# RWKV operands: a block's intermediate values in PSUM, affine steps on ScalarE

## The chip, the cores and the metric

The kernel runs on one core of a Trainium2 chip. The time is device microseconds from the start of the program to its end on that core; lower is better. Five engines work side by side: PE (TensorE, matrix products), DVE (VectorE), ACT (ScalarE), POOL (GpSimd) and SP (SyncE, which issues the transfers). Each takes its instructions in its own fixed order and waits for semaphores that others raise. SBUF is the on-chip memory of all engines, PSUM the one that PE writes its products to; in this kernel PSUM is eight banks of 128 partitions x 512 floats.

## The reference, cut to what matters

One layer of a hybrid backbone: one input projection feeds three branches, mLSTM, RWKV-7 and RG-LRU, whose results are gated and projected out. There are 2304 tokens of width 1024: 256 of context and 2048 of latent. The change concerns what RWKV needs for each token before its recurrence can run:

```
log_w = -RWKV_DECAY_SCALE * sigmoid(r_w0 + einsum('btdr,drc->btdc', tanh(wl), r_w2))
a     = sigmoid(r_a0 + einsum('btdr,drc->btdc', al, r_a2))
kt    = k * (1.0 + (a - 1.0) * r_ka)
bvec  = kh * a
# then, per head and direction, token by token:
S = S * w - (S kh) b + v kt;   y = S r        # w = exp(log_w)
```

The kernel runs the recurrence in chunks of 64 tokens. For that it needs, in each chunk, the running sum of log_w (its exponential is called E here, its inverse cs), and kh, r, b and kt multiplied by E or by its inverse. sigmoid(x) is computed as 0.5 tanh(x/2) + 0.5.

## The kernel before, in words

The program is written as generators that a small planner (class `Flow`) runs on an estimated clock. A generator issues its instructions and yields a delay or an event; the planner picks the next one by rank and due time. The order of PE's instructions is the order in which the planner reached them. The order on the other engines is that of a list scheduler, within the dependencies; semaphores are placed from the dependencies between tiles. All PSUM tiles of the program come from one pool `ps` of eight banks, which are handed on in turn, so that a new tile waits until the last reader of an older one is done. PE fills the time between the branches' work with the input projection (tiles `pp_...`).

`derive()` (L833 to L1063) makes the RWKV operands. There are 54 blocks of 256 tokens of one head pair and direction, in 7 stages (6 blocks in the first, 8 in each other one). Three `worker()` generators (`NW` = 3) take blocks in turn, and the tile `KB`, which holds a block's four results, has three buffers. For one block, `block()` does the following.

- PE: `pw`, four matmuls of 256 columns into one PSUM bank: the decay's argument in the first half, a's in the second.
- ACT: Tanh of each half into `KB` (L950, L952).
- DVE: the affine step 0.5 x + 0.5 into `cs` (L955), then the scan, the running sum over each chunk (L956).
- ACT: E = exp(-cs) into `E` (L957), one of two tiles with a column of ones ahead of each chunk, and the inverse into `cs` (L958).
- The a's half, scaled and shifted by two pointers, becomes two parts of `KB`: one on DVE (L959), one on ACT (L960).
- DVE: four products: `KB` halves by z (L965, 512 columns), kh by E (L967), r by E (L969 forward, L971 backward), and both halves by the inverse (L972, 512 columns).
- SP: three transfers of `KB` to the array `CH` in DRAM; ACT: a copy of E's last column into `Dall` (L977).

After a planned delay the worker lets PE multiply parts of the block with each other (`pt`, 16 matmuls), and ACT reads the bank six times into `DG` and `OF` (L1007 to L1009). When the blocks of a stage are in, DVE transposes `DG` into `W` (L1049), and POOL solves 32 triangular systems by a recursion of 30 steps of two instructions (L1058, L1060), masked at its start (L1050). DVE transposes the result back (L1030, L1031) and copies it (L1034), and PE and ACT merge it (`pY`, L909, `pX`, L918) before it goes to `CH`. When the last stage is merged, `derive()` is over and the mLSTM branch begins.

Of the kernel before, what the change touches and what calls it, by code (L numbers as in the profile page):

```python
# [9 lines left out]
F32 = mybir.dt.float32  # L10
F32R = mybir.dt.float32r
BF16 = mybir.dt.bfloat16
AF = mybir.ActivationFunctionType
ALU = mybir.AluOpType
# [11 lines left out]
DECAY = 0.6065306597126334  # L26
# [806 lines left out]
def derive(X, dv):  # L833
    nc, vec, hv, CH, F = X["nc"], X["vec"], X["hv"], X["CH"], X["F"]
    V = _VI
    NW, LOAD, LAT = 3, 10000.0, 11000.0
    sm = dv.tile([128, 256], BF16, name="sm")
# [5 lines left out]
    for s, (on, off) in enumerate(((slice(0, 64), slice(64, 128)), (slice(64, 128), slice(0, 64)))):  # L843
        nc.vector.memset(ab[on, 2 * s:2 * s + 2], 0.5)
        nc.vector.tensor_scalar(ab[off, 2 * s], ka[off], 0.5, None, op0=ALU.mult)
        nc.vector.tensor_scalar(ab[off, 2 * s + 1], ka[off], -0.5, 1.0, op0=ALU.mult, op1=ALU.add)
    Es = []
    for i in range(2):
        Es.append(dv.tile([128, 4, 65], F32, name=f"E{i}"))
        nc.gpsimd.memset(Es[i][:, :, 0:1], 1.0)  # L850
    CP = TP // 64
# [5 lines left out]
    n, per = 256, 4  # L857
# [16 lines left out]
    taken = [Event() for _ in stages]  # L874
    ahead, cnt = [], [0]

# [52 lines left out]
    def block():  # L929

        _, sid, p, d, i0, l0, nm, wa, z = ahead.pop(0)
        E = Es[cnt[0] % 2]
        cnt[0] += 1
        bw = d == 1
# [8 lines left out]
        def tok(x):  # L943

            v = x.rearrange("p (c j) -> p c j", j=64) if len(x.shape) == 2 else x
            return v[:, ::-1, ::-1] if bw else v
        sa = KB[:, :, 0]
        sw = KB[:, :, 1]
        i = V[f"w0_{d}{p}"]
        nc.scalar.activation(sw, pw[:, 0].rearrange("p (c j) -> p c j", j=64), AF.Tanh, scale=0.5, bias=hv[:, i:i + 1])  # L950
        i = V[f"a0_{d}{p}"]
        nc.scalar.activation(sa, pw[:, 1].rearrange("p (c j) -> p c j", j=64), AF.Tanh, scale=0.5, bias=hv[:, i:i + 1])  # L952
        cf = dv.tile([128, 256], F32, tag="cs", name=f"cs{nm}", bufs=2)
        cs = cf.rearrange("p (c j) -> p c j", j=64)
        nc.vector.tensor_scalar(cs, tok(sw), 0.5, 0.5, op0=ALU.mult, op1=ALU.add)  # L955
        nc.vector.tensor_tensor_scan(out=cf, data0=sm, data1=cf, initial=0.0, op0=ALU.mult, op1=ALU.add)  # L956
        nc.scalar.activation(E[:, :, 1:65], cs, AF.Exp, scale=-DECAY)  # L957
        nc.scalar.activation(cs, cs, AF.Exp, scale=DECAY)  # L958
        nc.vector.tensor_scalar(KB[:, :, 2], tok(sa), ab[:, 0, p:p + 1], ab[:, 1, p:p + 1], op0=ALU.mult, op1=ALU.add)  # L959
        nc.scalar.activation(KB[:, :, 3], tok(sa), AF.Identity, scale=ab[:, 2, p:p + 1], bias=ab[:, 3, p:p + 1])  # L960
        z4 = z[:, 2:4].rearrange("p a (c j) -> p c a j", j=64)
        if bw:
            z4 = z4[:, ::-1, :, ::-1]
        k = KB[:, :, 2:4]
        nc.vector.tensor_tensor(out=k, in0=k, in1=z4, op=ALU.mult)  # L965
        kh, r3 = tok(z[:, 0]), z[:, 1].rearrange("p (c j) -> p c j", j=64)
        nc.vector.tensor_tensor(out=KB[:, :, 1], in0=E[:, :, 0:64], in1=kh, op=ALU.mult)  # L967
        if bw:
            nc.vector.tensor_tensor(out=KB[:, :, 0], in0=E[:, :, 64:0:-1], in1=r3[:, ::-1], op=ALU.mult)  # L969
        else:  # L970
            nc.vector.tensor_tensor(out=KB[:, :, 0], in0=E[:, :, 1:65], in1=r3, op=ALU.mult)  # L971
        nc.vector.tensor_tensor(out=k, in0=cs[:, :, None].to_broadcast([128, 4, 2, 64]), in1=k, op=ALU.mult)  # L972
        ch = CH[p, d][:, i0:i0 + per].rearrange("p c (a j) -> p c a j", j=64)
        nc.sync.dma_start(ch[0:64, :, 2:6], KB[0:64])
        nc.sync.dma_start(ch[64:128, :, 0:2], KB[64:128, :, 2:4])
        nc.sync.dma_start(ch[64:128, :, 2:4], KB[64:128, :, 0:2])
        nc.scalar.activation(X["Dall"][:, p, d, i0:i0 + per], E[:, :, 64], AF.Copy)  # L977
        if d:
# [992 lines left out]
```

## Time and profile before

| | us |
|---|---|
| median of 3 runs | 2057.64 (2053.56 to 2067.47) |
| the profiled execution, its time | 2059.59 |
| its span on the core | 2057.9 |
| PE busy in the span | 1801.6 (88%) |
| DVE busy | 1367.0 (66%) |
| ACT busy | 977.6 (48%) |
| POOL busy | 795.0 (39%) |
| blocks of `derive()`, first scan to last product | 644 to 968 |

The span is that of one execution taken by the hardware profiler. An engine is busy while it executes an instruction; waiting is idle time. A row that says that A waited for B names what ended the wait last. In the order rows below, a bracket names the queues and engines whose semaphores an instruction waits for; Activation is ACT.

### The profile page before, as it was taken

The page shows a single profiled execution, that of the slowest core. Times are in us where ns is not written, and L with a number is a line of the kernel's source. Part 1 is how long each engine was busy: PE and PEld are TensorE (multiplying, and loading weights), DVE is VectorE, ACT ScalarE, POOL GpSimd, SP SyncE. Part 2 cuts the span into 40 slices and gives each one's busy share as a digit, 9 for nine tenths or more (in the row PEclk, how much of TensorE's full clock was granted, in tenths as well). Part 3 has the DMA queues.
Part 4 walks back from the last instruction along what each step waited for, and adds up shares of the span by engine and source line. Part 5 has one row for each costly group of instructions (what it writes and reads, how often), then busy time and mean ns, then how long its engine had stood idle before and what let it go on. Part 6 is the DMA issues. An engine that isn't in the chain of part 4 may idle for free. (4 is left out here: it accounts for less than half of the span.)

```text
span 2057.9 us, 46221 instructions
## 1 busy us (share of the span) xinstructions
PE 1801.6 (88%) x16648; PEld 1201.0 (58%) x16778; DVE 1367.0 (66%) x3271; ACT 977.6 (48%) x2634; POOL 795.0 (39%) x1200
## 2 busy tenths in 40 slices
PE   5899999999999878788899798878778788999996
PEld 3555655656666556555566565555555556777774
DVE  3747366777643898998324766647885576777774
ACT  5732446565434667776242545542332233444442
POOL 0210011112110688888722444342653232444442
PEclk9899999999999988889999899989888999999997
DMA  7343344564548778887254666645986545576662
GB/s 284 118 142 90 126 123 133 153 168 148 132 127 247 215 207 223 225 214 176 80 154 135 188 171 170 171 118 154 292 268 193 164 136 149 163 196 203 197 190 72
DMA packets 353370, 350.60 MB, mean 170 GB/s; under 512 B 109554, under 2 KB 294978, under 8 KB 350728
## 3 DMA queue, kind: packets, MB, share of 16 engines
q1 hardware_dynamic: 353142, 347.65, 59.2%
q8 instruction: 133, 2.18, 0.5%
q14 instruction: 95, 0.78, 0.1%
HBM read 211.18 MB, written 136.37 MB: 169 GB/s over the span
## 5 line engine op out<-in xcount | busy, mean ns | idle before, releaser
L1635 POOL TENSOR_SCALAR sd<-cg,Dall 128x128 f32<-128x128 f32 x210 | 135.8, 654 | 267.1 <-DVE cg L1659 164.0
L1659 DVE SCALAR_TENSOR_TENSOR cg<-cq,Dall,sd 64x64 f32<-64x64 f32 x408 | 114.5, 281 | 46.4 <-PE cq L168 36.6
L1060 POOL TENSOR_TENSOR W<-W,tmp 128x30 f32<-128x30 f32 (+14 forms) x210 | 139.0, 662 | 16.1
L1058 POOL TENSOR_TENSOR tmp<-W 128x30 f32<-128x30 f32 (+14 forms) x210 | 133.0, 633 | 15.9
L168 PE MATMUL cq<-cg,bt 128*64 128x64 f32 x840 | 68.5, 246 | 49.7 <-DVE cg L1644 44.6
L1283 ACT ACTIVATE nb<-nb,aT 128x128 f32<-128x128 f32 x216 | 71.6, 393 | 82.5 <-DMA nb<-nm_d 72.4
L168 PE MATMUL cq<-cg 128*64 128x64 f32 x1728 | 92.9, 230 | 8.2 <-DVE cg L1659 8.2
L168 PEld LDWEIGHTS cq<-cg,bt 128*64 128x64 f32 x840 | 44.1, 142 | 84.9 <-DVE cg L1644 54.8
L168 PE MATMUL ga<-cg 64*64 64x128 f32 (+1 forms) x864 | 76.9, 270 | 16.9 <-DMA cg<-ch 16.9
L1630 ACT ACTIVATE q<-cq 128x64 f32<-128x64 f32 x216 | 45.5, 223 | 95.7 <-PE cq L168 92.3
L1592 DVE TENSOR_TENSOR cg<-gb,rmask 64x256 f32<-64x256 f32 x108 | 44.7, 413 | 66.3 <-PE gb L168 61.1
L168 PEld LDWEIGHTS cq<-cg 128*64 128x64 f32 x1728 | 72.9, 141 | 24.3 <-issue 9.5
L168 PE MATMUL pz<-owhi,zhi 128*128 128x512 f32 x180 | 82.1, 456 | 4.5 <-ACT zhi L1822 4.5
L1598 ACT ACTIVATE bt<-ga 128x256 f32<-128x256 f32 x108 | 41.3, 383 | 87.0 <-DVE G L1595 83.4
L168 PE MATMUL pt<-KB 64*64 64x64 f32 x864 | 41.9, 244 | 45.7 <-DVE KB L972 45.6
L1284 POOL TENSOR_SCALAR_AFFINE_SELECT nb<-nb 128x256 f32<-128x256 f32 x108 | 44.8, 421 | 93.0 <-ACT nb L1283 63.6
L168 PE MATMUL gb<-cg 64*64 64x128 f32 (+1 forms) x864 | 75.7, 270 | 0.9 <-DMA cg<-ch 0.9
L168 PE MATMUL pz<-owhi,zlo 128*128 128x512 f32 x180 | 73.5, 409 | 3.3 <-DVE zlo L1823 3.3
L168 PE MATMUL pz<-owlo,zhi 128*128 128x512 f32 x180 | 72.9, 405 | 0.0
L168 PEld LDWEIGHTS ga<-cg 64*64 64x64 f32 x864 | 48.2, 142 | 41.9 <-issue 27.9
L168 PE MATMUL cq<-q,cg 128*64 128x64 f32 x864 | 59.4, 236 | 9.9 <-ACT q L1630 9.9
L168 PE MATMUL pp_v<-hhi,whi_v 128*128 128x512 f32 (+1 forms) x120 | 67.4, 562 | 0.3 <-ACT whi_v L514 0.3
(511 smaller groups left out, 6180.0 us busy)
## 6 DMA issues: line engine op xcount, KB each, us to landing
cg<-ch SPq DMA_DIRECT2D x216, 192.0 KB
wa<-wa SPq DMA_DIRECT2D x54, 256.0 KB
z<-z SPq DMA_DIRECT2D x27, 512.0 KB
ch<-KB SPq DMA_DIRECT2D x108, 128.0 KB
ch<-KB SPq DMA_DIRECT2D x54, 256.0 KB
nb<-nm_d SPq DMA_DIRECT2D x108, 128.0 KB
lr<-L SPq DMA_DIRECT2D x16, 768.0 KB
lL<-lr SPq DMA_DIRECT2D x16, 768.0 KB
```

The costliest lines, as they stand in the source:

```text
L168: self.nc.tensor.matmul(out, lhsT, rhs, start=start, stop=stop, **kw)
L1058: nc.gpsimd.tensor_tensor(out=tv, in0=W[:, j + 1:32, j:j + 1].to_broadcast([128, m, j]), in1=W[:, j:j + 1, 0:j].to_broadcast([128, m, j]), ...
L1060: nc.gpsimd.tensor_tensor(out=W[:, j + 1:32, 0:j], in0=W[:, j + 1:32, 0:j], in1=tv, op=ALU.add)
L1283: nc.scalar.activation(nb[:, d, j], nb[:, d, j], AF.Exp, bias=aT[:, c, d, 2 * p + j:2 * p + j + 1])
L1284: nc.gpsimd.affine_select(out=nb[:, d], in_=nb[:, d], pattern=[[0, 2], [1 - 2 * d, 128]], base=0, channel_multiplier=-1 + 2 * d, compare_o ...
L1592: nc.vector.tensor_tensor(out=cg[o, :, RK[h]], in0=src[o], in1=mask[o, d].rearrange("p a c -> p (a c)")[:, None].to_broadcast([64, 2, 128] ...
L1598: nc.scalar.activation(bt, ga[:, 1], AF.Copy)
L1630: nc.scalar.activation(q, qk, AF.Copy, scale=-1.0)
L1635: nc.gpsimd.tensor_scalar(sd, cg.rearrange("p (n c) -> p n c", c=64)[:, 0::9], Dk, None, op0=ALU.mult)
L1659: nc.vector.scalar_tensor_tensor(out=nxt[h][b], in0=ps[b], scalar=Dk[b], in1=sd[b, 1 - h], op0=ALU.mult, op1=ALU.add)
```

## The change

A block's intermediate values stay in PSUM. Both Tanh write in place into `pw`, the affine step is an ACT instruction of its own on that bank (L945 of the changed kernel), the scan reads it (L950), and E replaces the decay's half of `pw` (L956). Both ka-steps run on ACT, from `pw` into a new PSUM tile `kb` (L954, twice), in which DVE multiplies by z (L961); the last product reads `cs` from SBUF and `kb` from PSUM into `KB` (L969). So each DVE product has one operand in PSUM. The tiles E0 and E1 with their columns of ones go; the product of kh by E is now 63 columns of each chunk (L964), and the first column is copied (L963). `Dall` is read from `pw` (L974). PE's matmuls, the transfers, the stages, the workers and the planner's delays are as before, and PE's instructions stand in the same order.

```diff
--- before.py
+++ after.py
@@ -844,10 +844,6 @@
         nc.vector.memset(ab[on, 2 * s:2 * s + 2], 0.5)
         nc.vector.tensor_scalar(ab[off, 2 * s], ka[off], 0.5, None, op0=ALU.mult)
         nc.vector.tensor_scalar(ab[off, 2 * s + 1], ka[off], -0.5, 1.0, op0=ALU.mult, op1=ALU.add)
-    Es = []
-    for i in range(2):
-        Es.append(dv.tile([128, 4, 65], F32, name=f"E{i}"))
-        nc.gpsimd.memset(Es[i][:, :, 0:1], 1.0)
     CP = TP // 64
 
     stages = [[(p, d, 0, CP, CP * (2 * p + d)) for p in range(3) for d in range(2)]]
@@ -872,7 +868,7 @@
     full = [Event() for _ in stages]
     merged = [Event() for _ in stages]
     taken = [Event() for _ in stages]
-    ahead, cnt = [], [0]
+    ahead = []
 
     def load(lat=LOAD):
 
@@ -929,8 +925,6 @@
     def block():
 
         _, sid, p, d, i0, l0, nm, wa, z = ahead.pop(0)
-        E = Es[cnt[0] % 2]
-        cnt[0] += 1
         bw = d == 1
         pw = X["ps"].tile([128, 2, 256], F32, tag="b", name=f"pw{nm}")
         for j in range(2):
@@ -944,37 +938,40 @@
 
             v = x.rearrange("p (c j) -> p c j", j=64) if len(x.shape) == 2 else x
             return v[:, ::-1, ::-1] if bw else v
-        sa = KB[:, :, 0]
-        sw = KB[:, :, 1]
+
+        sw, sa = pw[:, 0], pw[:, 1]
         i = V[f"w0_{d}{p}"]
-        nc.scalar.activation(sw, pw[:, 0].rearrange("p (c j) -> p c j", j=64), AF.Tanh, scale=0.5, bias=hv[:, i:i + 1])
+        nc.scalar.activation(sw, sw, AF.Tanh, scale=0.5, bias=hv[:, i:i + 1])
+        nc.scalar.activation(sw, sw, AF.Copy, scale=0.5, bias=0.5)
         i = V[f"a0_{d}{p}"]
-        nc.scalar.activation(sa, pw[:, 1].rearrange("p (c j) -> p c j", j=64), AF.Tanh, scale=0.5, bias=hv[:, i:i + 1])
+        nc.scalar.activation(sa, sa, AF.Tanh, scale=0.5, bias=hv[:, i:i + 1])
         cf = dv.tile([128, 256], F32, tag="cs", name=f"cs{nm}", bufs=2)
         cs = cf.rearrange("p (c j) -> p c j", j=64)
-        nc.vector.tensor_scalar(cs, tok(sw), 0.5, 0.5, op0=ALU.mult, op1=ALU.add)
-        nc.vector.tensor_tensor_scan(out=cf, data0=sm, data1=cf, initial=0.0, op0=ALU.mult, op1=ALU.add)
-        nc.scalar.activation(E[:, :, 1:65], cs, AF.Exp, scale=-DECAY)
-        nc.scalar.activation(cs, cs, AF.Exp, scale=DECAY)
-        nc.vector.tensor_scalar(KB[:, :, 2], tok(sa), ab[:, 0, p:p + 1], ab[:, 1, p:p + 1], op0=ALU.mult, op1=ALU.add)
-        nc.scalar.activation(KB[:, :, 3], tok(sa), AF.Identity, scale=ab[:, 2, p:p + 1], bias=ab[:, 3, p:p + 1])
+        nc.vector.tensor_tensor_scan(out=cf, data0=sm, data1=sw[:, ::-1] if bw else sw, initial=0.0, op0=ALU.mult, op1=ALU.add)
+        k = X["ps"].tile([128, 4, 2, 64], F32, tag="b", name=f"kb{nm}")
+        sat = tok(sa)
+        for s in range(2):
+            nc.scalar.activation(k[:, :, s], sat, AF.Identity, scale=ab[:, 2 * s, p:p + 1], bias=ab[:, 2 * s + 1, p:p + 1])
+        E = sw.rearrange("p (c j) -> p c j", j=64)
+        nc.scalar.activation(sw, cf, AF.Exp, scale=-DECAY)
+        nc.scalar.activation(cf, cf, AF.Exp, scale=DECAY)
         z4 = z[:, 2:4].rearrange("p a (c j) -> p c a j", j=64)
         if bw:
             z4 = z4[:, ::-1, :, ::-1]
-        k = KB[:, :, 2:4]
         nc.vector.tensor_tensor(out=k, in0=k, in1=z4, op=ALU.mult)
         kh, r3 = tok(z[:, 0]), z[:, 1].rearrange("p (c j) -> p c j", j=64)
-        nc.vector.tensor_tensor(out=KB[:, :, 1], in0=E[:, :, 0:64], in1=kh, op=ALU.mult)
+        nc.vector.tensor_copy(KB[:, :, 1, 0:1], kh[:, :, 0:1])
+        nc.vector.tensor_tensor(out=KB[:, :, 1, 1:64], in0=E[:, :, 0:63], in1=kh[:, :, 1:64], op=ALU.mult)
         if bw:
-            nc.vector.tensor_tensor(out=KB[:, :, 0], in0=E[:, :, 64:0:-1], in1=r3[:, ::-1], op=ALU.mult)
+            nc.vector.tensor_tensor(out=KB[:, :, 0], in0=E[:, :, ::-1], in1=r3[:, ::-1], op=ALU.mult)
         else:
-            nc.vector.tensor_tensor(out=KB[:, :, 0], in0=E[:, :, 1:65], in1=r3, op=ALU.mult)
-        nc.vector.tensor_tensor(out=k, in0=cs[:, :, None].to_broadcast([128, 4, 2, 64]), in1=k, op=ALU.mult)
+            nc.vector.tensor_tensor(out=KB[:, :, 0], in0=E, in1=r3, op=ALU.mult)
+        nc.vector.tensor_tensor(out=KB[:, :, 2:4], in0=cs[:, :, None].to_broadcast([128, 4, 2, 64]), in1=k, op=ALU.mult)
         ch = CH[p, d][:, i0:i0 + per].rearrange("p c (a j) -> p c a j", j=64)
         nc.sync.dma_start(ch[0:64, :, 2:6], KB[0:64])
         nc.sync.dma_start(ch[64:128, :, 0:2], KB[64:128, :, 2:4])
         nc.sync.dma_start(ch[64:128, :, 2:4], KB[64:128, :, 0:2])
-        nc.scalar.activation(X["Dall"][:, p, d, i0:i0 + per], E[:, :, 64], AF.Copy)
+        nc.scalar.activation(X["Dall"][:, p, d, i0:i0 + per], E[:, :, 63], AF.Copy)
         if d:
             load()
         return sid, l0, nm, KB
```

ACT's queue at block 1_10241 (stage 1), before; `pY` belongs to the merge of the stage before:

```order
L950 ACTIVATE KB_1_10241_7548<-pw_1_10241_7543,hv 128x4x64 [waits DMAHW5_49,DMAHW6_49,DMAHW2_49,PE_49]
L952 ACTIVATE KB_1_10241_7548<-pw_1_10241_7543,hv 128x4x64
L960 ACTIVATE KB_1_10241_7548<-KB_1_10241_7548,rab 128x4x64 [waits Activation_49]
L957 ACTIVATE E_5316<-cs_1_10241_7551 128x4x64 [waits DVE_49]
L958 ACTIVATE cs_1_10241_7551<-cs_1_10241_7551 128x256 [waits Activation_49]
L977 ACTIVATE Dall<-E_5316 128x4
L909 ACTIVATE OF_6058<-pY_7474 32x512 [waits PE_49]
L909 ACTIVATE OF_6058<-pY_7474 32x512
```

After, at the same block:

```order
L944 ACTIVATE pw_1_10241_7597<-pw_1_10241_7597,hv 128x256 [waits PE_49]
L945 ACTIVATE pw_1_10241_7597<-pw_1_10241_7597 128x256 [waits Activation_49]
L947 ACTIVATE pw_1_10241_7597<-pw_1_10241_7597,hv 128x256 [waits Activation_49]
L954 ACTIVATE kb_1_10241_7608<-pw_1_10241_7597,rab 128x4x64 [waits DVE_49]
L954 ACTIVATE kb_1_10241_7608<-pw_1_10241_7597,rab 128x4x64 [waits Activation_49]
L956 ACTIVATE pw_1_10241_7597<-cs_1_10241_7606 128x256 [waits Activation_49]
L957 ACTIVATE cs_1_10241_7606<-cs_1_10241_7606 128x256 [waits Activation_49]
L974 ACTIVATE Dall<-pw_1_10241_7597 128x4 [waits DVE_49]
L905 ACTIVATE OF_6072<-pY_7528 32x512 [waits PE_49]
```

The ka-step has moved from ahead of the scan's result to behind it (L960 waited for ACT alone, the first L954 waits for DVE), each instruction now waits for the one ahead of it, and the copy into `Dall` waits for DVE.

DVE's queue at the same block, before:

```order
L955 TENSOR_SCALAR cs_1_10241_7551<-KB_1_10241_7548 128x256 [waits Activation_49]
L959 TENSOR_SCALAR KB_1_10241_7548<-KB_1_10241_7548,rab 128x4x64 [waits DMAHW5_49,DMAHW2_49,DMAHW6_49,PE_49,Activation_49]
L956 SCALAR_TENSOR_TENSOR cs_1_10241_7551<-sm,cs_1_10241_7551 128x256 [waits DVE_49]
L965 TENSOR_TENSOR KB_1_10241_7548<-KB_1_10241_7548,z_1_1024_7295 128x4x128 [waits DVE_49,Activation_49]
L967 TENSOR_TENSOR KB_1_10241_7548<-E_5316,z_1_1024_7295 128x4x64 [waits Activation_49]
L969 TENSOR_TENSOR KB_1_10241_7548<-E_5316,z_1_1024_7295 128x4x64
L972 TENSOR_TENSOR KB_1_10241_7548<-cs_1_10241_7551,KB_1_10241_7548 128x4x128 [waits DVE_49,Activation_49]
```

After:

```order
L963 COPY KB_1_10241_7602<-z_1_1024_7343 128x4 [waits DMAHW5_49,DMAHW6_49,DMAHW4_49,PE_49]
L950 SCALAR_TENSOR_TENSOR cs_1_10241_7606<-sm,pw_1_10241_7597 128x256 [waits Activation_49]
L961 TENSOR_TENSOR kb_1_10241_7608<-kb_1_10241_7608,z_1_1024_7343 128x512 [waits Activation_49]
L964 TENSOR_TENSOR KB_1_10241_7602<-pw_1_10241_7597,z_1_1024_7343 128x4x63 [waits Activation_49]
L966 TENSOR_TENSOR KB_1_10241_7602<-pw_1_10241_7597,z_1_1024_7343 128x4x64
L969 TENSOR_TENSOR KB_1_10241_7602<-cs_1_10241_7606,kb_1_10241_7608 128x4x128 [waits DVE_49,Activation_49]
```

The affine step and the ka-step are gone, the small copy has come in ahead of the scan, and the scan reads `pw`.

PE's queue between two blocks of stage 1, before (`pt` of one block, then `pw` of a later one, then the projection again):

```order
L168 MATMUL pp_mq_3_7819<-hlo,w_mq_6659 128x512
L168 MATMUL pt_1_12800_7913<-KB_1_12800_7646 64x64 [waits DVE_49,PE_49]
L168 MATMUL pt_1_12800_7913<-KB_1_12800_7646 64x64 x7
L168 MATMUL pw_1_15361_7930<-wa_1_15361_7568,w_0_20481_6918 128x256 [waits DMAHW7_49,PE_49,Activation_49]
L168 MATMUL pw_1_15361_7930<-wa_1_15361_7568,w_0_20481_6918 128x256 x3
L168 MATMUL pp_mq_3_7819<-hhi,whi_mq_7174 128x512
```

After:

```order
L168 MATMUL pp_mq_3_7881<-hlo,w_mq_6691 128x512
L168 MATMUL pt_1_12800_7975<-KB_1_12800_7702 64x64 [waits Activation_49]
L168 MATMUL pt_1_12800_7975<-KB_1_12800_7702 64x64 x7
L168 MATMUL pw_1_15361_7992<-wa_1_15361_7624,w_0_20481_6956 128x256 [waits DMAHW2_49,DVE_49]
L168 MATMUL pw_1_15361_7992<-wa_1_15361_7624,w_0_20481_6956 128x256 x3
L168 MATMUL pp_mq_3_7881<-hhi,whi_mq_7220 128x512
```

The instructions are the same; the waits are others: `pt` waits for ACT, which must first have read the bank's former tile, and `pw` waits for DVE in place of ACT, the bank's former tile being one that DVE's products read.

## Rows read from the trace of the kernel before

**Rows 1.** the page of the profile: the span of the one core, and its instructions

```profile
span 2057.9 us, 46221 instructions
```

**Rows 2.** windows: start and end, length, busy us of each engine, clock, DMA

```profile
core 0: us, PE busy (x) PEld busy (x) DVE busy (x) ACT busy (x) POOL busy (x), PEclk, DMA share, GB/s
640.00:980.00 340.00, 281.90 (x3040) 193.67 (x3077) 297.91 (x427) 240.35 (x743) 257.51 (x371) 0.87 0.81 215
700.00:940.00 240.00, 197.37 (x2261) 137.33 (x2286) 224.18 (x310) 172.99 (x534) 206.91 (x296) 0.85 0.83 220
980.00:1035.00 55.00, 46.32 (x553) 31.23 (x559) 17.43 (x19) 14.77 (x26) 40.25 (x78) 0.91 0.24 65
```

**Rows 3.** waits, 640 to 990 us: who waited for whom, total, times, longest

```profile
POOL W L1050 <- DVE W L1049: 62.5, 6, 55.2
ACT E L957 <- DVE cs L956: 54.6, 22, 6.4
PE pt L168 <- DVE KB L972: 45.6, 22, 5.7
PE pY L168 <- DVE XT L1031: 11.1, 2, 5.8
```

**Rows 4.** DVE's scan and products, line by line: minimum, median, maximum ns; first, last start

```profile
L956 DVE TENSOR_TENSOR_SCAN cs<-sm,cs x54: 672/679/1139, 644.0 to 964.0; 128x256 f32<-128x256 bf16 x54
...
L965 DVE TENSOR_TENSOR KB<-KB,z x54: 658/884/1730, 645.8 to 965.2; 128x512 f32<-128x512 f32 x54
...
L967 DVE TENSOR_TENSOR KB<-E,z x54: 383/596/920, 647.3 to 965.9; 128x256 f32<-128x256 f32 x54
...
L972 DVE TENSOR_TENSOR KB<-cs,KB x54: 661/914/1178, 649.2 to 967.4; 128x512 f32<-128x512 f32 x54
```

**Rows 5.** POOL, 700 to 940 us: times, busy us, mean ns, idle before

```profile
L1060 POOL TENSOR_TENSOR W<-W,tmp 128x240 f32<-128x240 f32 x10 | 9.2, 917 | 0.8
```

**Rows 6.** POOL, the same add from 985 to 1030 us

```profile
L1060 POOL TENSOR_TENSOR W<-W,tmp 128x240 f32<-128x240 f32 x2 | 1.3, 674 | 0.2
```

**Rows 7.** the transpose ahead of a stage's recursion, columns as in Rows 4

```profile
L1049 DVE STREAM_TRANSPOSE W<-DG x7: 1916/1996/2076, 680.1 to 972.3; 128x1024 f32<-128x1024 f32 x7
```

**Rows 8.** timeline of DVE from 985: start us, us, instruction, idle before it

```profile
985.96 1.91 DVE L1030 STREAM_TRANSPOSE XT<-W 128x1024 f32<-128x1024 f32 x1 [3.99 <-POOL W L1060]
987.73 2.06 DVE L1031 STREAM_TRANSPOSE XT<-W 128x1024 f32<-128x1024 f32 x1
...
990.39 1.40 DVE L1034 COPY XT<-XT 32x1024 f32<-32x1024 f32 x2
...
1025.09 1.92 DVE L1030 STREAM_TRANSPOSE XT<-W 128x1024 f32<-128x1024 f32 x1 [2.44 <-POOL W L1060]
```

**Rows 9.** timeline of ACT over one block, columns as in Rows 8

```profile
811.68 0.47 ACT L950 ACTIVATE KB<-pw,hv 128x256 f32<-128x256 f32 x1
812.06 0.47 ACT L952 ACTIVATE KB<-pw,hv 128x256 f32<-128x256 f32 x1
812.55 0.60 ACT L960 ACTIVATE KB<-KB,rab 128x256 f32<-128x256 f32 x1
813.83 0.42 ACT L957 ACTIVATE E<-cs 128x256 f32<-128x256 f32 x1 [0.68 <-DVE cs L956]
814.28 0.42 ACT L958 ACTIVATE cs<-cs 128x256 f32<-128x256 f32 x1
814.60 0.19 ACT L977 ACTIVATE Dall<-E 128x4 f32<-128x4 f32 x1
```

**Rows 10.** ACT by form, whole span: PSUM to SBUF, then SBUF to PSUM

```profile
L823 ACT ACTIVATE vs<-pv 128x256 f32<-128x256 f32 x6 | 2.3, 380 | 3.5 <-PE pv L175 3.5
...
L1450 ACT ACTIVATE lpr<-L 128x256 f32<-128x256 f32 x4 | 1.5, 366 | 0.0
```

**Rows 11.** PE by group, 640 to 980 us: the matmuls of pw and pt

```profile
L168 PE MATMUL pw<-wa,w 128*128 128x256 f32 x208 | 44.1, 340 | 7.0 <-DMA wa<-wa 5.5 <-DMA w<-w 1.5
L168 PE MATMUL pt<-KB 64*64 64x64 f32 x864 | 41.9, 244 | 45.7 <-DVE KB L972 45.6 <-issue 0.2
```

## The prediction

> **What bounds the kernel now.** I read the program's own span first [rows 1], then busy time by engine in the stretch where `block()` runs, then who waits for whom there, then single instructions. In the 340 us from 640 to 980 no engine is full [rows 2]: DVE works 297.9, PE 281.9, POOL 257.5, ACT 240.4. In the steady middle, 700 to 940, DVE works 224.2 of 240 us (93%), and it is what the others wait for [rows 3]: ACT 54.6 us for the scan (L956), PE 45.6 us for the last product (L972) and 11.1 us for a transpose. So DVE, one block after another, sets the pace. The blocks' scans start at 644.0 us and the last of the 54 at 964.0 [rows 4], so one block comes every (964.0 - 644.0) / 53 = 6.04 us. POOL's 62.5 us of waiting is one wait of 55.2 before the first stage and little after it; from 700 to 940 its recursion is at work in 206.9 of 240 us.
>
> DVE is full partly because its instructions are long. Scan and products take 0.679, 0.884, 0.596 and 0.914 us at the median and 0.672, 0.658, 0.383 and 0.661 at the least [rows 4]. POOL sees the same: one of its adds of 128x240 takes 917 ns in the middle [rows 5] and 674 ns when DVE is nearly idle [rows 6]. The two engines hold each other up when both work from SBUF.
>
> The end of the stretch belongs to POOL. The seventh stage's input transpose (L1049) starts at 972.3 [rows 7], but its recursion starts when the sixth is done, shortly before the transpose of the sixth's result at 985.96, and ends shortly before that of its own at 1025.09 [rows 8]: 39.1 us. In 980 to 1035 PE works 46.3 of 55 us [rows 2], so a shorter tail can give at most 55 - 46.3 = 8.7 us.
>
> **What leaves DVE.** One affine step (L955) and one scaled ka-step (L959) per block go to ACT, a copy of 128x4 comes (bound: nothing to the 0.383 of a 128x256 product, ten or more times as large; I take 0.1). What is left is scan, two products of 128x512, one of 128x256 and one of 63 columns in four groups. At the least durations of [rows 4] that is 0.67 + 0.66 + 0.66 + 0.38 + 0.38 + 0.1 = 2.85 us a block; with medians 3.77. Either is far under 6.04, so DVE stops being the bound, and POOL, freed of the contention, needs 39.1 us for a stage of eight blocks instead of about 48 (6.04 x 8).
>
> **What comes to ACT.** Before, the block's six instructions stand from 811.68 to 814.79 with 0.68 of waiting for the scan [rows 9]: 3.11 - 0.68 = 2.43 us; independent neighbours start before the one ahead has ended (L952 0.38 after L950). After there are eight. No row shows ACT reading and writing PSUM, so I bound it: PSUM to SBUF of 128x256 takes 380 ns, SBUF to PSUM 366 [rows 10], SBUF to SBUF 0.42 (L957); each end in PSUM saves about 0.04, and PSUM to PSUM would be 0.38 + 0.366 - 0.42 = 0.33. The upper bound is the SBUF price. A bias pointer costs 0.47 - 0.38 = 0.09 (L950 against the plain read), two cost 0.60 - 0.42 = 0.18. Thus two Tanh 0.43 each, affine 0.33, two ka-steps 0.33 + 0.18 = 0.52 each, E 0.37, its inverse 0.41, Dall 0.19: 3.20. Each now works on what the one ahead has just written or on its bank, so nothing overlaps, and a hand-over of 0.03 (L957 ends 814.25, L958 starts 814.28) comes seven times: 3.41. That is 0.98 more a block, 54 x 0.98 = 53 us; at the upper bound (SBUF prices throughout) 0.09 + 2 x 0.08 + 0.05 + 2 x 0.04 = 0.38 more a block, 20 us in all, and I take the lower price, since both rows with one end in PSUM lie under the SBUF one.
>
> **The waits that the change adds.** ACT takes its instructions in order. The first ka-step (L954) writes from the bank that the scan reads, and waits for the scan; the scan waits for the second Tanh (L947), which writes the same bank. In 45 of the 54 blocks the order has nothing between L947 and L954 on ACT, so ACT idles 0.04 + 0.68 + 0.03 = 0.75 us: 34 us. Behind the waiting L954 stand E, its inverse, Dall and then the next block's Tanh or the six reads of `pt`, for which PE and DVE wait. Second, Dall (L974) now reads the bank that DVE's products L964 and L966 read, and waits for the second of them: 0.38 + 0.41 less the 0.41 of L957 beside them, with a semaphore on either side 0.45 to 0.8; I take 0.6. In 23 blocks nothing stands between: 14 us. Before, Dall waited for nobody. The Trainium skill's page "PSUM — Partial Sum Buffer", section "PSUM bank collisions raise a hardware error", says that two engines may not touch one bank in the same partitions at once, even to read it; that is why Dall waits here at all, and it speaks against keeping a chain of two engines in one bank. No run here shows the error itself.
>
> **The sum.** ACT in 640 to 980: 240 busy + 53 + 34 + 14 = 341 us, so the stretch is full of ACT with its new waits alone. DVE's long instructions come on top, as ACT now depends on DVE twice a block: an L1049 (2.0), L1030 (1.9), L1031 (2.1) and two L1034 (1.4) [rows 7, 8], 7.4 us a stage, 7 of the first and 5 of each other here: 7 x 2.0 + 5 x 5.4 = 41 us. A quarter, 10 us, lies on the path, since ACT waits for DVE in 1.35 of some 6 us. Then ACT's other waits, mostly for PE: before 340 - 240 - 55 = 45 us; they shrink where ACT comes last, and I keep 18 of them (0 to 45 possible). 341 + 10 + 18 = 369 against 340: +29. In the tail POOL is no longer behind, so the last recursion starts at once: 985.96 - (972.3 + 2.0) = 11.7 us earlier, of which PE's work leaves 8.7. Net +20: 2059.59 of the profiled run (2057.9 span and 1.7 around it) gives **2080 us**. That run lies 2 us above the median of 2057.64, and the median's spread is 2053.56 to 2067.47, so about 1% is what a measurement can tell from no change.
>
> Hidden: two POOL memsets and the smaller E buffers (no row of the stretch rests on them); the wait for the old KB's transfers moves from L950 to the small copy L963 ahead of the scan, so it reaches ACT as before. If L963 is late, scan and ACT are late by as much.
>
> **Rivals.** *A, the relief wins.* If ACT's waits on DVE are covered by other ACT work, DVE and POOL run at their least durations, and what PE waits for them, 45.6 + 11.1 = 56.7 us, goes by half or more: 2059.6 - 28 = 2031; with all of PE's idle time, 340 - 281.9 = 58.1, it ends at 2001. It decides if ACT needs less than 6.04 us a block with its waits; the sum has 341 / 54 = 6.31, close to it. For it speak the contended durations, against it the order on ACT. Chance 0.22. The Trainium skill's page "SBUF — State Buffer", section "Who interferes with whom", states this mechanism: a DVE instruction with two SBUF inputs locks out GpSimd's reads for its whole length, one with at most one does not. By that rule every product here stops contending; the trace agrees with the contention (917 against 674 ns), and by the rule alone the time would be case A's.
>
> *B, nothing comes of it.* Waits are half covered and PE's waits move from DVE to ACT unchanged: 369 falls to 345 or 350, the tail gives its 8.7: 2056 to 2062. Chance 0.15.
>
> *C, PSUM banks tie PE to the chain.* All of `pw`, `kb`, `pt` and the projection share eight banks; a block now holds two of them until its last product. In the new order pt of a block waits for ACT's last read of the next block, and `pw` for DVE's last product two blocks back, where before `pw` waited for a Tanh only. If PE and ACT then alternate, a block costs ACT's 6.31 and PE's pw and pt, 44.1 / 52 + 41.9 / 54 = 0.85 + 0.78 [rows 11]: 7.9 us, +1.9 x 54 = +101. In half of the blocks: +50 - 8.7, so 2101. It decides once fewer than three blocks are in flight. Chance 0.15.
>
> **How the numbers follow.** My forecast has 0.48, with 2067 to 2097 as its own range (18 us of kept waits taken as 5 or 35; half of it lies beyond +1%, 2078). Faster: A, and a little of B, 0.23. Slower: half of mine and C, 0.39. Within 1%: the rest, 0.38. The range takes in most of A and of C: 2030 to 2105.
>
> **What would show it.** Right: in the blocks' stretch ACT waits some 35 us for the scan at the first L954 and some 14 at L974; PE waits for ACT rather than for DVE; the products fall to about 0.66 and 0.4 us, DVE's share to under 65%, POOL waits at L1050 between stages and its 128x240 add falls towards 674; blocks come every 6.4 to 6.7 us. Wrong: ACT idle at L954 in few blocks (A), `pt` and `pw` late by banks with ACT idle too (C), ACT's PSUM-to-PSUM instructions at 0.42 or more.

## The result, and the profile after

The changed kernel takes 2131.6 us at the median of 4 runs (2128.36 to 2136.57) against 2060.95 for the kernel before, now 4 runs too. The ratio on record is 1.0332, 95% interval 1.0307 to 1.0358 (the quotient of the two medians is 1.0343). The profiled execution has a span of 2134.8 us against 2057.9 [rows 1], 76.9 more. So it is slower, as forecast, but the loss is 71 us where 20 were forecast, and it lies above the range.

Where it lies is told by three DVE instructions. Lines of single instructions of the changed kernel (minimum, median and maximum in ns, then first and last start):

```profile
L950 DVE TENSOR_TENSOR_SCAN cs<-sm,pw x54: 641/686/708, 644.5 to 1046.8; 128x256 f32<-128x256 bf16 x54
...
L969 DVE TENSOR_TENSOR KB<-cs,kb x54: 674/677/706, 647.8 to 1050.9; 128x512 f32<-128x512 f32 x54
...
L1027 DVE STREAM_TRANSPOSE XT<-W x7: 1897/1930/2003, 739.5 to 1103.1; 128x1024 f32<-128x1024 f32 x7
```

The scans still start at 644.5 (before 644.0), but the last product starts at 1050.9 instead of 967.4: the blocks take 83.0 us more, 7.59 us each by the scans, where they took 6.04. From there to the last transpose it is 52.2 us, before 57.7: the tail gives 5.5 back. What follows it is 1.1 us shorter. 0.5 + 83.0 - 5.5 - 1.1 = 76.9.

Windows of the changed kernel up to its last product and of the kernel before up to its own (engines in the order PE, PEld, DVE, ACT, POOL, then granted clock and DMA):

```profile
640.00:1051.00 411.00, 296.50 (x2989) 198.95 (x3023) 204.06 (x366) 287.68 (x829) 200.36 (x379) 0.78 0.67 172
```

```profile
640.00:968.00 328.00, 270.58 (x2979) 186.86 (x3014) 293.15 (x423) 234.52 (x727) 246.68 (x354) 0.86 0.80 215
```

No engine is full after the change: PE 72%, ACT 70%, DVE 50%, POOL 49%. ACT works 287.7 - 234.5 = 53.2 us more, as the sum had it. PE has the same matmuls to do (some 10 apart) and is idle 114.5 us in place of 57.4; besides, its own work takes 25.9 us more, at a granted clock of 0.78 instead of 0.86. 57.1 + 25.9 is the 83 us of the two windows' lengths.

What PE waits for has changed altogether. Its longest waits in the changed kernel, 640 to 1060 us (what waited, for whom, total, times, longest):

```profile
PE pp_mk L168 <- ACT Dall L974: 19.1, 1, 19.1
PE pp_mk L168 <- ACT DG L1006: 16.7, 2, 13.7
PE pw L168 <- ACT DG L1006: 12.4, 3, 8.8
PE pw L168 <- ACT Dall L974: 10.1, 7, 5.5
PE pp_zl L168 <- ACT Dall L974: 9.4, 1, 9.4
PE pp_zl L168 <- ACT DG L1006: 5.4, 2, 3.5
PE pp_mq L168 <- DVE KB L969: 5.4, 1, 5.4
```

Before [rows 3] PE waited for data: `pt` for the last product, `pY` for a transpose. After, a matmul of the projection waits for the copy into Dall or the reads into DG, from which it takes nothing. What it needs of them is the PSUM bank that they read last. Taking from the full list the 4.5 us that are data or issue, 110 of 115 us are waits for a bank; none were before.

Whose banks they are is told by the reader that PE waits for. Over the full list 50.9 us are for Dall, the last reader of a `pw` bank, 40.1 for DG, the last reader of a `pt` bank, 11.6 for a copy of the projection's own results, and only 5.6 for L969, the last reader of `kb`. So PE hardly waits for kb's bank itself: kb takes a place in the turn, and the banks of `pw` and `pt` come up again while ACT has not yet read them. (PE takes its matmuls in order, so a wait for kb can hide behind an earlier one; the releasers alone do not show how much.)

The waits of ACT and DVE in the same stretch of the changed kernel:

```profile
ACT kb L954 <- DVE cs L950: 69.2, 51, 16.7
ACT Dall L974 <- DVE KB L966: 11.7, 13, 5.3
ACT Dall L974 <- DVE KB L968: 7.8, 13, 1.6
```

```profile
DVE cs L950 <- ACT pw L947: 61.2, 29, 8.0
...
DVE XT L1027 <- POOL W L1057: 14.3, 1, 14.3
DVE XT L1027 <- DMA ch<-XT: 11.5, 3, 7.7
```

ACT waits 69.2 us for the scan and 19.5 at Dall. DVE is ahead of all of it, but sits 25.8 us before L1027, the transpose of POOL's result (14.3 for POOL, 11.5 for a transfer): behind it in DVE's queue stand the scans.

One knot in the timeline of the changed kernel shows how these hang together (start, duration, engine and line, in brackets the idle time before it and its releaser), of ACT, POOL, DVE and PE in turn:

```profile
728.44 0.45 ACT L947 ACTIVATE pw<-pw,hv 128x256 f32<-128x256 f32 x1
745.60 1.11 ACT L954 ACTIVATE kb<-pw,rab 128x256 f32<-128x256 f32 x2 [16.71 <-DVE cs L950]
...
749.59 0.15 ACT L974 ACTIVATE Dall<-pw 128x4 f32<-128x4 f32 x1
```

```profile
739.23 0.25 POOL L1057 TENSOR_TENSOR W<-W,tmp 128x30 f32<-128x30 f32 x1
```

```profile
739.51 1.90 DVE L1027 STREAM_TRANSPOSE XT<-W 128x1024 f32<-128x1024 f32 x1 [14.29 <-POOL W L1057]
...
744.88 0.69 DVE L950 TENSOR_TENSOR_SCAN cs<-sm,pw 128x256 f32<-128x256 bf16 x1
```

```profile
749.80 0.80 PE L168 MATMUL pp_mk<-hhi,whi_mk 128*128 128x512 f32 x1 [19.12 <-ACT Dall L974]
```

L1027 stands before the scan of a block whose second Tanh was done at 728.9. DVE waits for POOL until 739.5, does the transposes, scans at 744.9; ACT goes on at 745.6, reads Dall at 749.6, and at 749.8 PE gets the bank for the next matmul of a projection that has nothing to do with RWKV. PE has stood still for 19.1 us.

DVE's work and the contention went as forecast: the products of 512 columns take 714 and 681 ns at the mean and 699 and 677 at the median (884 and 914 at the median before, [rows 4]), and POOL's add of 128x240 takes 675 (917 before, [rows 5]). Rows by line, of DVE and then of POOL over the stretch (times, busy us, mean ns, idle before):

```profile
L961 DVE TENSOR_TENSOR kb<-kb,z 128x512 f32<-128x512 f32 x54 | 38.5, 714 | 58.4 <-ACT kb L954 58.4
...
L969 DVE TENSOR_TENSOR KB<-cs,kb 128x512 f32<-128x512 f32 x54 | 36.8, 681 | 8.0 <-ACT cs L957 7.8
...
L1057 POOL TENSOR_TENSOR W<-W,tmp 128x240 f32<-128x240 f32 x14 | 9.4, 675 | 1.1
```

By the Trainium skill, "SBUF — State Buffer", section "Who interferes with whom", a DVE instruction with at most one SBUF input, outside the modes in which it uses two ports, does not contend with GpSimd, and the trace agrees with it: 675 ns against 917. No run below shows that it bought time.

### The profile page after: what moved, and what is told of

It reads as the page before. It is cut to its first block, busy times and chain, and to the rows that moved or that the text cites. A ratio compares the mean times of both kernels' runs of the same rounds, so it can differ in the third digit from the quotient of the medians.

```text
span 2134.8 us, 46128 instructions
## 1 busy us (share of the span) xinstructions
PE 1822.3 (85%) x16648; PEld 1208.2 (57%) x16778; DVE 1274.7 (60%) x3217; ACT 1034.5 (48%) x2742; POOL 735.6 (34%) x1198
## 3 DMA queue, kind: packets, MB, share of 16 engines
q1 hardware_dynamic: 353142, 347.65, 57.7%
## 5 line engine op out<-in xcount | busy, mean ns | idle before, releaser
L1656 DVE SCALAR_TENSOR_TENSOR cg<-cq,Dall,sd 64x64 f32<-64x64 f32 x408 | 114.5, 281 | 46.2 <-PE cq L168 36.4
L1057 POOL TENSOR_TENSOR W<-W,tmp 128x30 f32<-128x30 f32 (+14 forms) x210 | 109.5, 522 | 16.5
L1055 POOL TENSOR_TENSOR tmp<-W 128x30 f32<-128x30 f32 (+14 forms) x210 | 103.0, 491 | 15.9
L168 PE MATMUL cq<-cg,bt 128*64 128x64 f32 x840 | 67.9, 244 | 45.3 <-DVE cg L1641 40.1
L168 PE MATMUL pp_mk<-hhi,whi_mk 128*128 128x512 f32 (+1 forms) x120 | 67.2, 560 | 35.9 <-ACT Dall L974 19.1
L954 ACT ACTIVATE kb<-pw,rab 128x256 f32<-128x256 f32 x108 | 58.0, 537 | 70.9 <-DVE cs L950 69.2
L168 PE MATMUL pp_mq<-hhi,whi_mq 128*128 128x512 f32 (+1 forms) x120 | 70.3, 586 | 10.4 <-DVE KB L969 5.4
L1047 POOL TENSOR_SCALAR_AFFINE_SELECT W<-W 128x1024 f32<-128x1024 f32 x7 | 8.9, 1266 | 190.7 <-DVE W L1046 190.7
L950 DVE TENSOR_TENSOR_SCAN cs<-sm,pw 128x256 f32<-128x256 bf16 x54 | 36.9, 683 | 61.8 <-ACT pw L947 61.2
```

The costliest lines, as they stand in the source:

```text
L168: self.nc.tensor.matmul(out, lhsT, rhs, start=start, stop=stop, **kw)
L950: nc.vector.tensor_tensor_scan(out=cf, data0=sm, data1=sw[:, ::-1] if bw else sw, initial=0.0, op0=ALU.mult, op1=ALU.add)
L954: nc.scalar.activation(k[:, :, s], sat, AF.Identity, scale=ab[:, 2 * s, p:p + 1], bias=ab[:, 2 * s + 1, p:p + 1])
L1055: nc.gpsimd.tensor_tensor(out=tv, in0=W[:, j + 1:32, j:j + 1].to_broadcast([128, m, j]), in1=W[:, j:j + 1, 0:j].to_broadcast([128, m, j]), ...
L1057: nc.gpsimd.tensor_tensor(out=W[:, j + 1:32, 0:j], in0=W[:, j + 1:32, 0:j], in1=tv, op=ALU.add)
L1656: nc.vector.scalar_tensor_tensor(out=nxt[h][b], in0=ps[b], scalar=Dk[b], in1=sd[b, 1 - h], op0=ALU.mult, op1=ALU.add)
```

## The experiments

Each ratio is against the kernel before, run beside it. "The blocks take" is from the first scan's start to the last product's end: 324.5 us before, 407.0 after the change.

**The bank kb taken out again.** `kb_in_sbuf`:

```diff
-        k = X["ps"].tile([128, 4, 2, 64], F32, tag="b", name=f"kb{nm}")
+        k = KB[:, :, 2:4]
```

> The changed kernel with one thing put back: the two ka-steps write into the SBUF tile KB again, so a block takes one PSUM bank less, and DVE's two products of 512 columns have both operands in SBUF. ACT's instructions, their order within a block and both waits for DVE (at the first ka-step and at Dall) stay. Theory banks (the bank kb, handed on in turn with those of PE, makes PE wait for the chains of later blocks; 109 us of PE's waiting after the change is for a bank's last reader, none before): most of the 71 us comes back, PE's waits for banks fall under 50 us, the blocks take 325 to 350 us instead of 407, time 2060 to 2085. Theory chain (ACT's longer serial work with its two waits for DVE sets the pace whatever the banks): the blocks still take over 380 us, time 2110 to 2130. DVE's products of 512 columns go back towards 0.85 us in both.

2058.5 us, 0.9987 (0.9965 to 1.0009): the whole loss is gone. The blocks take 329.9 us. PE's waits in the run:

```profile
PE pt L168 <- DVE KB L969: 61.7, 20, 9.4
PE pY L168 <- DVE XT L1028: 3.6, 2, 3.4
PE pw L168 <- DMA w<-w: 1.0, 1, 1.0
```

They are for data again, as before the change. ACT does the same work as in the changed kernel and still waits 22.4 us at Dall, so its 53 us and that wait, beside what DVE is relieved of, cost nothing on balance. For the scan it waits only 16.0 us: 53 of the 69 us go with the bank. The products of 512 columns took 788 and 784 ns at the mean, not quite back to the 0.85 us that were expected. DVE is no fuller than after the change (215 of 334 us from 640 to 974), and the time is that of the kernel before.

**The bank kb added alone.** `before_kb_in_psum` is the kernel before with:

```diff
-        nc.vector.tensor_scalar(KB[:, :, 2], tok(sa), ab[:, 0, p:p + 1], ab[:, 1, p:p + 1], op0=ALU.mult, op1=ALU.add)
-        nc.scalar.activation(KB[:, :, 3], tok(sa), AF.Identity, scale=ab[:, 2, p:p + 1], bias=ab[:, 3, p:p + 1])
+        k = X["ps"].tile([128, 4, 2, 64], F32, tag="b", name=f"kb{nm}")
+        nc.vector.tensor_scalar(k[:, :, 0], tok(sa), ab[:, 0, p:p + 1], ab[:, 1, p:p + 1], op0=ALU.mult, op1=ALU.add)
+        nc.scalar.activation(k[:, :, 1], tok(sa), AF.Identity, scale=ab[:, 2, p:p + 1], bias=ab[:, 3, p:p + 1])
...
-        k = KB[:, :, 2:4]
...
-        nc.vector.tensor_tensor(out=k, in0=cs[:, :, None].to_broadcast([128, 4, 2, 64]), in1=k, op=ALU.mult)
+        nc.vector.tensor_tensor(out=KB[:, :, 2:4], in0=cs[:, :, None].to_broadcast([128, 4, 2, 64]), in1=k, op=ALU.mult)
```

> The kernel before with one part of the change alone: a new PSUM tile kb takes the two ka-steps (one on DVE, one on ACT, as before), and the products of 512 columns have one operand in it. ACT's work stays as before. Theory banks: one more bank per block, held to the last product, is enough to make PE wait: 2075 to 2110, with PE waiting for L972 or ACT's reads at tiles that have nothing to do with them. Theory chain: ACT has no more to do and DVE is relieved of contention in two of its five long instructions: 2035 to 2055, faster than before.

2074.8 us, 1.0079 (1.0052 to 1.0106), the blocks take 344.9: slower, at the lower end of what the banks were to cost. PE waits 9.4 us at `pw` for L1009 and 8.9 at a projection tile for a Tanh, both for banks, but most of all for data, the last product at `pt`. ACT also waits 64.0 us for L960, DVE's ka-step, which now writes the same bank as ACT's, and DVE 22.9 us at L1030 for POOL:

```profile
PE pt L168 <- DVE KB L972: 31.8, 8, 16.1
```

```profile
ACT kb L961 <- DVE kb L960: 64.0, 44, 20.5
```

So this run does not price the bank alone. What it does show is that kb in the common turn costs some 15 us on the kernel before, where `pw` is given back after the second Tanh, and over 70 on the changed kernel, where `pw` too is held until Dall; kb_in_sbuf holds `pw` as long without kb and loses nothing. So most of the loss needs kb in the turn and something else of the change beside it. Whether that is the longer hold of `pw` or ACT's new order, no run separates.

**ACT's waits for DVE taken away.** `no_waits_on_dve`:

```diff
-        nc.scalar.activation(sa, sa, AF.Tanh, scale=0.5, bias=hv[:, i:i + 1])
+        ta = dv.tile([128, 256], F32, tag="ta", name=f"ta{nm}", bufs=2)
+        nc.scalar.activation(ta, sa, AF.Tanh, scale=0.5, bias=hv[:, i:i + 1])
+        sa = ta
...
+        nc.scalar.activation(X["Dall"][:, p, d, i0:i0 + per], cs[:, :, 63], AF.Exp, scale=-DECAY)
         nc.scalar.activation(cf, cf, AF.Exp, scale=DECAY)
...
-        nc.scalar.activation(X["Dall"][:, p, d, i0:i0 + per], E[:, :, 63], AF.Copy)
```

> The changed kernel with ACT's two waits for DVE taken away by other data: the second Tanh writes an SBUF tile that the ka-steps read (so they need not wait for the scan that reads the pw bank), and Dall is a second exponential of 128x4 taken from the scan's result before the inverse overwrites it (so it need not wait for the products that read pw). The kb bank stays, pw is still held until the products by E. Theory chain: the 89 us that ACT waits for DVE (69 at the ka-steps, 20 at Dall) go, some 60 to 70% of the loss comes back: 2075 to 2095. Theory banks: PE still waits for banks that later blocks release; they are released a little sooner, 0.5 to 1 us a block, on a third of the blocks: 2105 to 2125.

2094.5 us, 1.0171 (1.0132 to 1.0210), the blocks take 363.7. Half of the loss: better than the banks alone had it, at the upper edge of what the chain had. The wait for the scan has moved to E, and PE waits 28.6 us (longest 17.2) and 19.9 at two projection tiles for DVE's products by E, now the last readers of `pw`:

```profile
PE pp_mk L168 <- DVE KB L971: 28.6, 2, 17.2
PE pp_zl L168 <- DVE KB L969: 19.9, 2, 13.7
```

```profile
ACT pw L958 <- DVE cs L952: 47.1, 41, 14.8
```

A shorter chain gives the bank back sooner; the waits are still for banks.

**A bank of its own for kb.** `kb_own_bank`:

```diff
-    X["ps"] = ctx.enter_context(tc.tile_pool(name="ps", bufs=8, space=PSUM))
+    X["ps"] = ctx.enter_context(tc.tile_pool(name="ps", bufs=7, space=PSUM))
+    X["kp"] = ctx.enter_context(tc.tile_pool(name="kp", bufs=1, space=PSUM))
...
-        k = X["ps"].tile([128, 4, 2, 64], F32, tag="b", name=f"kb{nm}")
+        k = X["kp"].tile([128, 4, 2, 64], F32, tag="k", name=f"kb{nm}")
```

> The changed kernel with kb in a PSUM pool of its own of one bank, and seven banks instead of eight for all others in the whole program, so that no tile of PE stands behind kb in the turn. ACT's and DVE's instructions stay. Theory banks: PE waits for banks less: the blocks' stretch shortens by 20 to 50 us, of which the seven banks elsewhere may take some back: 2080 to 2115. Theory chain: nothing in the stretch, 2125 to 2145. What the seven banks cost elsewhere is read from the time after the last block, 1083 us of the changed kernel's span.

2077.2 us, 1.0098 (1.0063 to 1.0134), the blocks take 342.7, and the time after the last product's end is no longer than in the changed kernel (1082.5 us against 1083.2), so no cost of the missing eighth bank shows there. The first of PE's waits:

```profile
PE pt L168 <- DVE KB L970: 66.9, 22, 7.8
PE pp_mq L168 <- DVE wlo_mq L517: 3.8, 1, 3.8
PE pY L168 <- DVE XT L1029: 1.4, 2, 0.9
```

With kb out of the common turn, PE's waits for banks are down to some 3 us though there are fewer banks for it, and 54 of the 71 us are back. ACT now waits 15.9 us for the one bank of kb.

**Both.** `own_bank_no_waits` joins the last two edits, no_waits_on_dve and kb_own_bank.

> kb_own_bank and no_waits_on_dve together: kb in a pool of one bank, seven banks for the rest, and ACT's two waits for DVE taken away by an SBUF tile for the second Tanh and by a second small exponential for Dall. Left of the change: ACT's longer work and DVE's products with one operand in PSUM. Theory banks plus chain: the 17 us that kb_own_bank still lost are the chain's, and go: 2045 to 2065. If ACT's work itself (53 us more) is what is left, it stays at 2070 to 2080.

2057.9 us, 0.9988 (0.9969 to 1.0006). The 17 us that were left go with the two waits. With all of the change's relief for DVE and POOL (692 and 677 ns, 672 ns) and all of its work on ACT, the time is that of the kernel before. PE still waits for the last product:

```profile
PE pt L168 <- DVE KB L973: 43.9, 14, 7.0
```

**The transpose put back.** `late_transpose` lets a copy of two columns from the newest block's KB go into the transpose's output first, so that L1027 stands behind that block. For the first stage 18 scans stand ahead of it, where 12 stood in the changed kernel and 16 before the change:

```diff
+    newest = [None]
...
+        newest[0] = KB
...
         with X["tc"].high_priority(offset=300):
+            nc.vector.tensor_copy(XT[:, 0, 31:33], newest[0][:, 0, 2, 0:2])
             nc.vector.transpose(XT[:, :, 0:32].rearrange("p l t -> p t l"), W)
```

> The changed kernel with the transpose of POOL's result (L1027) held back on DVE: a copy of 128x2 from the newest block's KB is written into the transpose's output first, so that L1027 stands behind that block's products, four blocks later for the first stage, where it stands before the change too. The banks' turn is as in the changed kernel. In the changed kernel DVE sat 25.8 us ahead of L1027 (14.3 for POOL, 11.5 for a transfer of the tile's former content). Theory banks alone: no more than those 26 us can come back, and less as PE's waits for banks stay: 2105 to 2125, the blocks' stretch still over 385 us. Theory transpose (the moved L1027 is the main cause, and kb_in_sbuf and kb_own_bank were quick because it stood later in them too): 2060 to 2090.

2114.6 us, 1.0271 (1.0246 to 1.0296), the blocks take 387.4. 17 us come back by the place of the transposes in DVE's order. It is a part of the loss, not its main cause.

**The bank alone.** `held_bank` is kb_in_sbuf with a bank that holds nothing of use:

```diff
+        hb = X["ps"].tile([128, 512], F32, tag="b", name=f"hb{nm}")
+        nc.scalar.activation(hb[:, 0:1], sa[:, 0:1], AF.Copy)
...
+        jk = dv.tile([128, 1], F32, tag="jk", name=f"jk{nm}", bufs=2)
+        nc.vector.tensor_tensor(out=jk, in0=hb[:, 0:1], in1=KB[:, 0, 2, 0:1], op=ALU.mult)
```

> kb_in_sbuf (2058.5 us) with nothing but a bank added: a PSUM tile per block from the common pool, of which ACT writes one column where the first ka-step stands and DVE reads that column behind the last product. The ka-steps' results stay in SBUF. The work added is a copy of one column on ACT (0.17 us or less each, as Dall's) and one on DVE, 54 of each, 9 us of ACT in all. Theory banks: the bank in the turn is the whole loss, so the time goes back to the changed kernel's or near it, 2105 to 2140, with PE waiting for ACT's reads and the last product of later blocks at tiles that don't need them. If the loss was another property of kb (where ACT writes, DVE's operands): 2060 to 2075.

2138.1 us, 1.0391 (1.0358 to 1.0423), the blocks take 410.8. From 2058.5 to 2138.1 by one column written and one read, with the waits of the changed kernel:

```profile
PE pp_mk L168 <- ACT Dall L978: 21.7, 1, 21.7
PE pp_mk L168 <- ACT DG L1010: 16.5, 2, 13.1
PE pw L168 <- ACT DG L1010: 12.2, 3, 8.7
PE pp_zl L168 <- ACT Dall L978: 10.4, 1, 10.4
PE pp_mq L168 <- ACT Dall L978: 10.4, 3, 5.0
```

This settles what was added: one more tile per block in the common turn, on top of the rest of the change, is the loss, whatever the tile holds. Here too PE waits 56.2 us for Dall and 40.9 for DG, but 5.5 for the read that ends the added tile. So that it is held until the last product may matter little; a tile soon given back was not tried. DVE's wait for POOL at the transpose came back with it (16.8 and 7.1 us), so something like the 17 us of late_transpose is in it.

**Where the relief can be spent.** `sbuf_kb_early_dall` is kb_in_sbuf with Dall taken early, as in no_waits_on_dve. The others change the planner's delay between `pw` and `pt`, to 14000 or, in `own_bank_lead_17`, to 17000: `sbuf_kb_more_lead` in sbuf_kb_early_dall, `before_more_lead` in the kernel before, `own_bank_lead_14` and `own_bank_lead_17` in own_bank_no_waits:

```diff
-    NW, LOAD, LAT = 3, 10000.0, 11000.0
+    NW, LOAD, LAT = 3, 10000.0, 14000.0
```

> kb_in_sbuf with Dall taken from the scan's result, so that it waits for no product. In kb_in_sbuf ACT waited 22.4 us for DVE at Dall. If ACT's waits for DVE are on the path there, 2040 to 2052; if PE's wait for the data of KB (61.7 us at pt) has other sources, 2053 to 2062.

> sbuf_kb_early_dall with the planner's delay between pw and pt of a block (LAT) at 14000 instead of 11000, so that more of the projection stands between them on PE. If what PE waits for there is only the length of the chain from pw to KB, PE's 62 us at pt fall by a half and the time to 2025 to 2045; if three blocks in flight give no more, the wait moves and the time stays at 2045 to 2065, as the last stage ends later.

> The kernel before with the planner's delay between pw and pt at 14000 instead of 11000, as the control for sbuf_kb_more_lead (2052.7). If DVE is full before the change, a longer lead buys nothing, 2055 to 2065; if PE's wait at pt is only the length of the chain, it gains as there, 2045 to 2055.

> own_bank_no_waits with the delay between pw and pt at 14000. There PE waited 44 us for KB at pt; if half goes as in sbuf_kb_more_lead (62 to 24), 2035 to 2050; if KB's buffers and their transfers (44 us of DVE's waiting at the small copy) hold it, 2050 to 2060.

> The same at 17000: PE's wait at pt nearly gone, but with three blocks in flight the blocks come later and the last stage ends later: 2035 to 2060, better than 14000 only if PE has enough of the projection left for the end.

| | us, median | ratio, 95% interval |
|---|---|---|
| sbuf_kb_early_dall | 2057.3 | 0.9986 (0.9967 to 1.0006) |
| sbuf_kb_more_lead (14000) | 2052.7 | 0.9968 (0.9953 to 0.9982) |
| before_more_lead (14000) | 2054.6 | 0.9997 (0.9980 to 1.0014) |
| own_bank_lead_14 | 2051.6 | 0.9968 (0.9949 to 0.9988) |
| own_bank_lead_17 | 2059.5 | 1.0007 (0.9985 to 1.0029) |

Taking Dall early bought nothing where banks were no issue. The longer lead cut PE's wait at `pt` from 61.5 us to 23.7 in the one pair, and from 43.9 to 23.0 in the other. DVE goes on waiting for KB's buffer to be sent off (24.9 us, before the longer lead 20.2, and 37.5, before it 43.9). Waits of PE and of DVE in own_bank_lead_14:

```profile
PE pt L168 <- DVE KB L973: 23.0, 15, 4.0
```

```profile
DVE KB L967 <- DMA ch<-KB: 37.5, 20, 5.7
```

The two best are 0.3% faster than the kernel before; their intervals leave out 1, but it is small. On the kernel before the same lead gave 2054.6 us, 2 to 3 us more than they took and within the spread of their runs, so that the change has a part in the 0.3% is not shown. There too PE's wait at `pt` fell, from 45.6 us to 17.8, and won next to nothing. In all three PE gains work up to 1100 us and loses most of it behind: 423.8 us from 640 to 1100 in own_bank_lead_14, against 395.9 in own_bank_no_waits, but 789.5 from 1100 to 2040, against 812.0. That the projection's matmuls, done sooner, are missing there to fill PE's waits is only argued. At 17000 the gain is gone.

## Why the prediction was wrong

- **What comes to ACT: right in size, in part by luck.** 53 us were forecast and 53.2 measured (rows of the instructions by line, changed kernel):

```profile
L954 ACT ACTIVATE kb<-pw,rab 128x256 f32<-128x256 f32 x108 | 58.0, 537 | 70.9 <-DVE cs L950 69.2
...
L944 ACT ACTIVATE pw<-pw,hv 128x256 f32<-128x256 f32 x54 | 24.1, 447 | 1.2
...
L956 ACT ACTIVATE pw<-cs 128x256 f32<-128x256 f32 x54 | 20.6, 382 | 1.2
...
L945 ACT ACTIVATE pw<-pw 128x256 f32<-128x256 f32 x54 | 19.9, 369 | 0.9
```

  Estimated were 0.52, 0.43, 0.37 and 0.33. Each is 1 to 4 hundredths longer. The 53 held hand-overs of 0.21 us a block, 11 us in all, which are idle time and no work. Measured, the block's instructions add up to 40 us more (138.5 us before, 178.5 after), and the rest is overlap between neighbours that is gone.
- **The sum: the step that failed.** It took ACT as the bound and added its waits to its work, 369 us in place of 340, and counted the banks at nothing. ACT worked 70% of the stretch, and a block came every 7.59 us where 6.4 to 6.7 were to show the forecast right. kb_in_sbuf has all that the sum counted, ACT's work and both of its waits, and loses nothing: what the sum priced costs nothing here, and what it left to rival C is the loss, 110 us of PE's waits for banks. The term "+34 us for the scan" measured 69.2, "+14 at Dall" 19.5, and kb_in_sbuf, with the same chain, has 16.0 of the 69.2, so that most of it was an effect of the stalled program and not its cause. A chain in one engine's queue was priced where a cycle over three engines was made: PE waits for a bank, the bank for Dall, Dall stands behind the wait for the scan, and a later block's scan waits for PE's `pw`.
- **Rival C was the mechanism and was under-priced.** It named the banks, and that `pt` waits for ACT's last read and `pw` for DVE's last product, with a chance of 0.15 and "half of the blocks", +50 and 2101 us. The blocks' loss was 83. Its picture was too narrow as well: it let PE and ACT alternate at `pw` and `pt`, while the largest single waits are of projection tiles, 19.1 and 13.7 us, which take their turn in the same banks; and `pw` waited for DG and Dall, 12.4 and 10.1 us, not for DVE's last product. The order of the changed kernel, with the new waits on `pt` and `pw`, had been read; what was not asked is what every other PSUM tile behind kb waits for.
- **A term that was missing: the transpose.** DVE's long instructions were given 10 us, as work. That L1027 had moved four blocks forward in DVE's queue for the first stage, and might itself wait for POOL, was not seen. DVE sat 25.8 us there in all; putting the transposes behind was worth 17.
- **A term that was missing: the clock.** PE's own matmuls took 25.9 us more; the granted clock was 0.78 in the stretch in place of 0.86.
- **The tail** gave 5.5 us of the 8.7. The last recursion did start at once, but POOL then stood 4.5 us for a copy of DVE's (L1031).
- **Rival A** had the relief right (714 and 681 ns, 675 ns) and its worth wrong: own_bank_no_waits has the relief, ACT's work and hardly any waits for banks, and ends at 0.9988, with PE still waiting 43.9 us at `pt`, where it waited 45.6 before [rows 3]. Whether the relief is worth nothing by itself, or what it gives is paid away by ACT's longer chain, stays open: no run has the one without the other or a held bank. The last part of the relief shows no worth: sbuf_kb_early_dall, with these products at 779 and 796 ns, took 2057.3 us, and own_bank_no_waits, with 692 and 677, took 2057.9 (the banks and the wait for the scan differ too). So the first part of the prediction, that DVE sets the pace, is not settled; against it speaks that DVE works three tenths less after the change (204 us in the stretch for 293) and that none of the runs with hardly any waits for banks is more than 0.3% faster.
- **The wait at Dall** was put down to the Trainium skill, "PSUM — Partial Sum Buffer", section "PSUM bank collisions raise a hardware error", by which two engines may not even read one bank in the same partitions at once. The trace agrees: Dall and the product ahead of it both only read `pw`, and ACT waits 19.5 us there. kb_own_bank leaves 17 us that go with this wait and the scan's. It was the smaller part.

## What to carry to other kernels

Before an intermediate value moves to PSUM, list every tile that takes its banks in the same turn, and ask of each what now releases its bank: one more tile per block, in a turn in which a slow chain already holds another, can stop the engine's work that has nothing to do with it. Read the new order for instructions that wait for a fourth engine in front of the chain's own. If the value must be in PSUM, a bank of its own cost less here than a place in the common turn, even with one bank less for the rest.

## What the runs showed of the hardware

ACT's exponential of 128x256 took 382 ns from SBUF to PSUM (L956) against 416 from SBUF to SBUF (L957), and its affine copy with both ends in PSUM 369. DVE's scan took about the same from PSUM as from SBUF (686 ns at the median, 679 before). The small copy of 128x4, forecast at 0.1 us, took 145 to 891 ns (its line in the changed kernel; minimum, median, maximum); that POOL's instructions hold it up is only argued:

```profile
L963 DVE COPY KB<-z x54: 145/165/891, 634.7 to 1041.1; 128x4 f32<-128x4 f32 x54
```

The granted clock stood at 0.78 in the changed kernel's stretch and at 0.79 in held_bank's, where PE waited most, and at 0.86 in kb_in_sbuf's and the kernel before's; as a mix of the two levels of 1.2 and 2.4 GHz, 0.78 is 56% of the time at the upper one and 0.86 is 72%. Whether PE's waiting alone lowers it was not tried.
